# Half B's late FFN pairs from seven block products, with weight sums made during half A's FFN

## The chip, the cores and the metric

The kernel runs on one core of a Trainium2 chip. The metric is the device time of one launch in microseconds (us), as the median of several runs.

## The reference, cut to what matters

One decoder layer is computed in fp32 for a prompt (1024 tokens) and eight short samples (8 x 4 tokens) that share weights. Two branches (RG-LRU and chunked gated linear attention) are merged; then comes the FFN, which the change touches:

```python
h2 = _rmsnorm(x, norm2_g) * (1.0 + sc2) + sh2
f1, f2 = jnp.split(h2 @ ffn_w1, 2, axis=-1)          # D_MODEL 1024 -> 2 x D_FF, D_FF = 2816
x = x + gt2 * ((jax.nn.silu(f1) * f2) @ ffn_w2)
```

## The kernel before, in words

Activations lie with features on the 128 partitions and tokens along the free axis. The tokens are worked in two halves one after the other: half A has 512 prompt tokens, half B has the other 512 and the 32 of the samples, 544. `B` keeps a product in two PSUM banks of 272 columns each. In names in the traces, `a` or `b` behind a tile's name is the half.

Every fp32 product is three fp32r matmuls (`gemm`, lines 355 to 357): high part of the weight by high part of the activation, high by low, low by high. Activations are stored as high and low part side by side in one tile. Weights come from DRAM on SyncE's queue (`load_raw`, three buffers) and are split when they arrive (`split_w`): ScalarE writes the high part (line 136), VectorE the difference (line 137), into an `hl` tile (three buffers). Splits are issued with raised priority (`AHEAD`), so that they stand some 70 instructions earlier than their place in the code.

The FFN has 22 pairs; `pair` (from line 1079) makes one block of 128 features of `f1` and of `f2`, each from eight 128-row blocks of `h2` (24 matmuls for each 512 or 272 columns). It then takes the tanh on ScalarE, two VectorE products, and the split of the result into an `fa` tile (ScalarE line 1099, VectorE line 1100). `back` runs the output projection, the second norm and the first eleven pairs, the first four of them (`EARLY`) on the two parts of the half separately (`ffn1_first`), the others on the whole (`ffn1`). Then `ffn2` runs: eight columns, each of 33 matmuls over the eleven `fa` tiles, with weights in two loads of six and five blocks. The second eleven pairs and the second `ffn2` follow in the main program.

What decides the order: the program is written as generators that are advanced in turn; a scheduler then lists the instructions of each engine by priority, as far as tiles are free. At run time each engine works its list strictly in order and waits on semaphores. Tiles come from pools: 17 `S` tiles (wide activations, `fa` among them), 6 `t` tiles (temporaries), one `m2t` tile, 3 `raw`, 3 `hl`; in PSUM half A has 6 tiles of one bank, half B 3 of two. GpSimd has little to do: a few products and copies in the branches, and outputs on its DMA queue (lines 788, 833, 1147).

## Time and profile before

| | us |
|---|---|
| median of 3 runs (2044.50 to 2046.26) | 2045.36 |
| the profiled execution | 2041.18 |
| its span in the trace | 2039.2 |

The page of the profile gives busy times and shares for each engine (PE is TensorE, PEld its weight loads, DVE VectorE, ACT ScalarE, POOL GpSimd, SP SyncE), then the span in 40 slices. Timeline rows give start, duration, engine, line, operation, tiles written and read, and in brackets how long the engine was idle before and what ended that. The stages that matter here, by the timeline: half A's first four FFN pairs on its first part end at about 653 us, its pairs on the whole begin at about 674, its first `ffn2` at about 750, its second eleven pairs end at about 930; half B's FFN begins at about 1655 us and runs to 2026 us.

### The profile page before, as it was taken

The numbers are of one execution on the slowest core, as the hardware profiler recorded it, in microseconds if no ns is written. First come the engines' busy times: TensorE is split into PE (matmuls) and PEld (weight loads), VectorE is DVE, ScalarE is ACT, GpSimd is POOL, SyncE is SP. The second block draws the span as 40 slices with busy tenths as digits, with TensorE's granted clock in tenths as the row PEclk, the third lists the DMA queues.
The fourth block names the chain that finished last, engine by engine and source line by source line (L and its number), as shares of the span: only waits on it lengthen the run. The fifth ranks groups of instructions, "written<-read, shape, count | busy, mean of one in ns | idle before, by whom it ended". The sixth has DMA issues, their size and how long they took to land. (4 is left out here: it accounts for less than half of the span.)

```text
span 2039.2 us, 31760 instructions
## 1 busy us (share of the span) xinstructions
PE 2005.9 (98%) x13306; PEld 1808.0 (89%) x13306; DVE 1096.8 (54%) x1768; ACT 799.0 (39%) x1117; POOL 76.1 (4%) x130
## 2 busy tenths in 40 slices
PE   8999999999999999999999999999999999999997
PEld 5887877777899888888899999999999999999997
DVE  5647586544358433446473597764334773333346
ACT  3534375533335322333352355653322442222232
POOL 0101001000000000000010011010000000000000
PEclk9999999999999999999999999999999999999998
DMA  8323223334344323232412312323233542232243
GB/s 305 105 92 125 88 94 116 102 119 159 93 153 158 124 78 119 93 132 84 149 63 87 126 53 94 109 89 104 73 92 108 177 134 87 72 105 93 82 121 123
DMA packets 74638, 228.39 MB, mean 112 GB/s; under 512 B 8704, under 2 KB 16768, under 8 KB 74496
## 3 DMA queue, kind: packets, MB, share of 16 engines
q1 hardware_dynamic: 71536, 217.38, 32.8%
q0 software_dynamic: 2416, 8.44, 1.1%
q8 instruction: 104, 1.70, 0.3%
q10 hardware_dynamic: 544, 0.56, 0.1%
q14 instruction: 38, 0.31, 0.0%
HBM read 217.11 MB, written 9.23 MB: 111 GB/s over the span
## 5 line engine op out<-in xcount | busy, mean ns | idle before, releaser
L357 PE MATMUL f3psb<-fab,f3b_hl 128*128 128x272 f32 x352 | 101.4, 288 | 0.0
L355 PE MATMUL f3psb<-fab,f3b_hl 128*128 128x272 f32 x352 | 101.3, 288 | 0.0
L356 PE MATMUL f3psb<-fab,f3b_hl 128*128 128x272 f32 x352 | 100.9, 287 | 0.0
L136 ACT ACTIVATE f3b_hl<-f3b_raw 128x768 fp32r<-128x768 f32 (+1 forms) x45 | 35.7, 793 | 88.6 <-PE f3psb L357 58.3
L355 PE MATMUL f3psa<-faa,f3a_hl 128*128 128x512 f32 x176 | 68.7, 390 | 0.0
L357 PE MATMUL f3psa<-faa,f3a_hl 128*128 128x512 f32 x176 | 68.5, 389 | 0.0
L356 PE MATMUL f3psa<-faa,f3a_hl 128*128 128x512 f32 x176 | 68.5, 389 | 0.0
L355 PEld LDWEIGHTS f3psb<-fab,f3b_hl 128*128 128x128 f32 x352 | 66.4, 189 | 0.0
L357 PEld LDWEIGHTS f3psb<-fab,f3b_hl 128*128 128x128 f32 x352 | 66.2, 188 | 0.0
L356 PEld LDWEIGHTS f3psb<-fab,f3b_hl 128*128 128x128 f32 x352 | 66.1, 188 | 0.0
L137 DVE TENSOR_TENSOR f3b_hl<-f3b_raw,f3b_hl 128x768 fp32r<-128x768 f32 (+1 forms) x45 | 40.1, 892 | 35.2 <-ACT f3b_hl L136 34.8
L136 ACT ACTIVATE f3a_hl<-f3a_raw 128x768 fp32r<-128x768 f32 (+1 forms) x32 | 25.4, 793 | 84.3 <-PE f3psa L357 47.9
L137 DVE TENSOR_TENSOR f3a_hl<-f3a_raw,f3a_hl 128x768 fp32r<-128x768 f32 (+1 forms) x32 | 28.5, 892 | 39.1 <-ACT f3a_hl L136 38.4
L355 PE MATMUL uxpsb<-h1b,uxpsb_hl 128*128 128x272 f32 x160 | 47.0, 293 | 0.1
L357 PE MATMUL uxpsb<-h1b,uxpsb_hl 128*128 128x272 f32 x160 | 46.4, 290 | 0.0
L355 PE MATMUL ugpsb<-h1b,ugpsb_hl 128*128 128x272 f32 x160 | 46.2, 289 | 0.0
L357 PE MATMUL ugpsb<-h1b,ugpsb_hl 128*128 128x272 f32 x160 | 46.1, 288 | 0.0
L356 PE MATMUL uxpsb<-h1b,uxpsb_hl 128*128 128x272 f32 x160 | 45.9, 287 | 0.0
L356 PE MATMUL ugpsb<-h1b,ugpsb_hl 128*128 128x272 f32 x160 | 45.8, 286 | 0.0
L357 PEld LDWEIGHTS f3psa<-faa,f3a_hl 128*128 128x128 f32 x176 | 33.0, 188 | 7.0 <-DVE f3a_hl L137 0.2
L356 PEld LDWEIGHTS f3psa<-faa,f3a_hl 128*128 128x128 f32 x176 | 33.0, 188 | 6.9
L355 PEld LDWEIGHTS f3psa<-faa,f3a_hl 128*128 128x128 f32 x176 | 33.0, 188 | 6.8
(1477 smaller groups left out, 7129.0 us busy)
## 6 DMA issues: line engine op xcount, KB each, us to landing
ada<-in_ada_w SPq DMA_DIRECT2D x48, 512.0 KB, 5.3
f3b_raw<-in_ffn SPq DMA_DIRECT2D x23, 384.0 KB, 3.1
f3b_raw<-in_ffn SPq DMA_DIRECT2D x22, 320.0 KB, 2.9
woa_raw<-in_w_out SPq DMA_DIRECT2D x13, 512.0 KB, 3.5
wob_raw<-in_w_out SPq DMA_DIRECT2D x13, 512.0 KB, 3.2
f3a_raw<-in_ffn SPq DMA_DIRECT2D x16, 384.0 KB, 3.1
uxpsa_raw<-in_w_in SPq DMA_DIRECT2D x10, 512.0 KB, 3.6
ugpsa_raw<-in_w_in SPq DMA_DIRECT2D x10, 512.0 KB, 3.6
```

Source lines behind the costliest of these rows:

```text
L136: act.activation(hl[:, 0, :n], raw[:, :n], AF.Copy)
L137: dve.tensor_sub(hl[:, 1, :n], raw[:, :n], hl[:, 0, :n].bitcast(F32))
L355: pe.matmul(out, wh, x[:, o:o + w], start=st, stop=False)
L356: pe.matmul(out, wh, x[:, N + o:N + o + w], start=False, stop=False)
L357: pe.matmul(out, wl, x[:, o:o + w], start=False, stop=en)
```

## The change

Half B's pairs from number 6 (`PLAIN`) on, sixteen of them, are made by `pair7`. A pair's weights are seen as 2 x 2 blocks (`f1` and `f2`, 128 outputs each, by two halves of 512 input rows), and `h2` as 2 x 2 blocks too (those halves by two halves of 272 tokens). Seven block products of 12 matmuls with 272 columns (four 128-row blocks times three parts) replace eight, by way of sums of weight blocks and of activation blocks:

- `make_sums` (32 steps, one for each of the 16 pairs and half of the columns) makes the four sums of weight blocks on GpSimd in the one `m2t` buffer, splits them (ScalarE line 187, VectorE line 188 of the new file) into two `S` tiles, and stores them to DRAM from GpSimd's queue. It is advanced during half A's FFN.
- `mixed` and `mixed_last` make the sums of `h2` blocks in half B, with three fourths of them during the first six pairs.
- `pair7` loads `qa` and `qe` on SyncE's queue and splits them as before (512 and 256 KB), and the stored sums `qc` (1 MB), `qb` and `qd` (512 KB each) on GpSimd's queue, which need no split. Products `x`, `y` share a PSUM tile of two banks (`xy`), `v`, `z` another (`wz`). In between, ScalarE and VectorE take what is done so far out of the banks (`e`, `u2`, `u4`, `f2`, `f12`).

```diff
@@ -28,6 +28,7 @@
 LEVELS = (64, 32, 16, 8, 4, 2, 1)
 EPS = 1e-6
 EARLY = 4
+PLAIN = 6
 AHEAD = 70
 def starts_of(w):
     return [min(i, w - P) for i in range(0, w, P)]
@@ -162,6 +163,31 @@
         def __getitem__(s, at):
             rows, u, cols = at
             return s.of[u][rows, cols]
+
+
+    dp = ctx.enter_context(tc.tile_pool(name="dp", bufs=1, space=bass.MemoryType.DRAM))
+    sums = {}
+
+    def make_sums(fs):
+
+        for f in fs:
+            sums[f] = dp.tile([P, 2, 4, 512], F32R, tag=f"sum{f}", name=f"sum{f}")
+            for i in range(2):
+                q = tp.tile([P, 2 * 544], F32, tag="m2t", name=f"sq{f}{i}", bufs=1)[:, :1024].rearrange("p (s n) -> p s n", s=4)
+                c = slice(256 * i, 256 * i + 256)
+                w = [I["ffn1"][2 * f + u].rearrange("p (k n) -> p k n", k=2)[:, :, c] for u in range(2)]
+                for u, k, at in (0, 0, 1), (0, 1, 3), (1, 0, 2), (1, 1, 0):
+                    pool.dma_start(q[:, at], w[u][:, k])
+                pool.tensor_add(q[:, 0], q[:, 2], q[:, 0])
+                pool.tensor_add(q[:, 2], q[:, 1], q[:, 2])
+                pool.tensor_add(q[:, 1], q[:, 1], q[:, 0])
+                pool.tensor_add(q[:, 3], q[:, 3], q[:, 1])
+                yield 0.0
+                hi, lo = (S(f"s{u}{f}{i}", F32R)[:, :1024].rearrange("p (s n) -> p s n", s=4) for u in "hl")
+                act.activation(hi, q, AF.Copy)
+                dve.tensor_sub(lo, q, hi.bitcast(F32))
+                for u, t in (0, hi), (1, lo):
+                    pool.dma_start(sums[f][:, u, :, c], t)
 
     def w_in_tile(t, name):
         return load_w(I["w_in"][t], 1024, name)
@@ -322,6 +348,7 @@
             s.parts = [(0, 256, 0, 0), (256, 256, 0, 256)] if hf == 0 else [(0, 272, 0, 0), (272, 272, 1, 0)]
             s.adas = ada_rest() if hf == 0 else iter(())
             s.early = {}
+            s.seven = s.hf == 1
             s.lr_raw = None
 
         def ada(s, n):
@@ -1100,6 +1127,108 @@
             dve.tensor_sub(lo, tg, hi.bitcast(F32))
             yield w * 24 / 2400.0
 
+        def mixed(s):
+
+            N, w = s.N, s.N // 2
+            s.t1, s.t2, s.t3, s.t4 = [], [], [], []
+            whole = lambda h, o, n: (h[:, o:o + n].bitcast(F32), h[:, N + o:N + o + n].bitcast(F32))
+            for j in range(4):
+                n = f"{s.n}{j}"
+                hs, gs = T("mh" + n), T("mg" + n)
+                dve.tensor_add(hs[:, :N], *whole(s.h2[j], 0, N))
+                dve.tensor_add(gs[:, :N], *whole(s.h2[4 + j], 0, N))
+                yield
+                h0, h1, g0, g1 = hs[:, :w], hs[:, w:N], gs[:, :w], gs[:, w:N]
+                dve.tensor_sub(h0, h0, h1)
+                dve.tensor_sub(h1, h1, g1)
+                dve.tensor_add(g1, h0, g1)
+                dve.tensor_sub(g0, g0, g1)
+                t34 = S("mt" + n, F32R)
+                if j % 2 == 0:
+                    t2 = S("mu" + n, F32R)
+                for dst, at, src, to in (t34, 0, h1, s.t3), (t34, N, g0, s.t4), (t2, j % 2 * N, g1, s.t2):
+                    split(dst[:, at:at + N], src, w)
+                    to.append((dst[:, at:at + w], dst[:, at + w:at + N]))
+                    yield
+
+        def mixed_last(s):
+            N, w = s.N, s.N // 2
+            for j in range(4):
+                h = s.h2[j]
+                hs = T(f"ml{s.n}{j}")
+                dve.tensor_add(hs[:, :N], h[:, :N].bitcast(F32), h[:, N:2 * N].bitcast(F32))
+                dve.tensor_sub(hs[:, :w], hs[:, :w], hs[:, w:N])
+                hi, lo = h[:, w:N], h[:, N + w:2 * N]
+                act.activation(hi, hs[:, :w], AF.Copy)
+                dve.tensor_sub(lo, hs[:, :w], hi.bitcast(F32))
+                s.t1.append((hi, lo))
+
+        def quarter(s, k0, c):
+            N, w = s.N, s.N // 2
+            return [(h[:, c * w:c * w + w], h[:, N + c * w:N + c * w + w]) for h in s.h2[k0:k0 + 4]]
+
+        def pair7(s, f, a):
+
+            n, N, w = f"{s.n}{f}", s.N, s.N // 2
+            d = sums[f]
+
+            def prod(out, hl, u, rhs, first, last):
+                for k, (xh, xl) in enumerate(rhs):
+                    c = u * 512 + k * P
+                    wh, wl = hl[:, 0, c:c + P], hl[:, 1, c:c + P]
+                    pe.matmul(out, wh, xh, start=(first and k == 0), stop=False, skip_group_check=True)
+                    pe.matmul(out, wh, xl, start=False, stop=False, skip_group_check=True)
+                    pe.matmul(out, wl, xh, start=False, stop=(last and k == 3), skip_group_check=True)
+
+            def load(at, name):
+                hl = wp.tile([P, 2, 1024], F32R, tag="hl", name=name + n + "_hl", bufs=3)
+                pool.dma_start(hl[:, :, :512 * len(at)].rearrange("p u (s n) -> p u s n", n=512), d[:, :, at.start:at.stop])
+                return hl
+
+            xy, wz = mm("xy" + n), mm("wz" + n)
+            x, y = (xy[:, 0, :w], xy[:, 1, :w]) if s.hf else (xy[:, 0, :w], xy[:, 0, w:N])
+            v, z = (wz[:, 0, :w], wz[:, 1, :w]) if s.hf else (wz[:, 0, :w], wz[:, 0, w:N])
+            eu, vf, tg, f2 = T("eu" + n), T("vf" + n), T("tg" + n), T("ff" + n)
+            e, u2 = eu[:, :w], eu[:, w:N]
+            u4, f12 = vf[:, :w], vf[:, w:N]
+            ha = load_w(I["ffn1"][2 * f], 1024, "qa" + n)
+            prod(x, ha, 0, s.quarter(0, 0), True, True)
+            with tc.high_priority(AHEAD + 20):
+                act.activation(e, x, AF.Copy)
+            hc = load(range(1, 3), "qc")
+            prod(y, hc, 0, s.t2, True, True)
+            with tc.high_priority(AHEAD + 20):
+                dve.tensor_sub(u2, y, e)
+            yield w * 24 / 2400.0
+            prod(x, ha, 1, s.quarter(4, 0), False, True)
+            prod(v, hc, 1, s.t3, True, True)
+            with tc.high_priority(AHEAD + 20):
+                dve.tensor_add(u4, u2, v)
+            act.activation(tg[:, :w], x, AF.Tanh, scale=0.5)
+            dve.scalar_tensor_tensor(tg[:, :w], tg[:, :w], 1.0, x, op0=OP.add, op1=OP.mult)
+            yield w * 24 / 2400.0
+            hb = load(range(0, 1), "qb")
+            raw = load_raw(I["ffn1"][2 * f + 1][:, 512:], 512, "qe" + n)
+            with tc.high_priority(AHEAD):
+                act.activation(hb[:, 0, 512:], raw[:, :512], AF.Copy)
+                dve.tensor_sub(hb[:, 1, 512:], raw[:, :512], hb[:, 0, 512:].bitcast(F32))
+            prod(z, hb, 0, s.t1, True, True)
+            with tc.high_priority(AHEAD + 20):
+                dve.tensor_sub(f2[:, w:N], u4, z)
+            prod(v, hb, 1, s.t4, False, True)
+            dve.tensor_add(f2[:, :w], u2, v)
+            yield w * 24 / 2400.0
+            hd = tp.tile([P, 2 * 544], F32R, tag="m2t", name="qd" + n, bufs=1)[:, :1024].rearrange("p (u n) -> p u n", u=2)
+            pool.dma_start(hd, d[:, :, 3])
+            prod(z, hd, 0, s.quarter(4, 1), False, True)
+            with tc.high_priority(AHEAD + 20):
+                dve.tensor_sub(f12, z, u2)
+            act.activation(tg[:, w:N], f12, AF.Tanh, scale=0.5)
+            dve.scalar_tensor_tensor(tg[:, w:N], tg[:, w:N], 1.0, f12, op0=OP.add, op1=OP.mult)
+            dve.tensor_mul(tg[:, :N], tg[:, :N], f2[:, :N])
+            split(a, tg[:, :N], N)
+            yield w * 12 / 2400.0
+
         def ffn1_first(s, part, n):
             for f in range(n) if part[0] == 0 else range(n - 1, -1, -1):
                 if part[0] == 0:
@@ -1111,7 +1240,7 @@
                 s.act = []
             for f in range(11 * g + f0, 11 * g + 11):
                 a = S(f"fa{s.n}{f}", F32R)
-                yield from s.pair(f, s.whole, a)
+                yield from s.pair7(f, a) if s.seven and f >= PLAIN else s.pair(f, s.whole, a)
                 s.act.append(a)
 
         def ffn2(s, g, part, acc=None):
@@ -1162,9 +1291,21 @@
             next(f)
             mix(s.norm2(p1, a1), f)
             drain(f)
-            drain(s.ffn1_first(p1, EARLY))
-            drain(s.ffn1(0, EARLY))
-            drain(s.ffn2(0, s.whole))
+            m = s.mixed() if s.seven else make
+            for _ in s.ffn1_first(p1, EARLY):
+                next(m, None)
+            f = s.ffn1(0, EARLY)
+            if s.seven:
+                for _ in range(2 * (PLAIN - EARLY)):
+                    next(f)
+                    for _ in range(3):
+                        next(m, None)
+                drain(m)
+                s.mixed_last()
+            for _ in f:
+                next(make, None)
+            for _ in s.ffn2(0, s.whole):
+                next(make, None)
 
         def branches(s, before):
             s.y_a, s.os_ = [None] * NR, []
@@ -1203,6 +1344,7 @@
         for _ in range(n):
             pe.matmul(idle, src[:, :P], src[:, :512], start=True, stop=True, skip_group_check=True)
 
+    make = make_sums(range(PLAIN, NF))
     A.begin()
     load_later()
     derive()
@@ -1210,6 +1352,8 @@
     up1 = A.ffn1(1)
     for _ in range(16):
         next(up1)
+        next(make, None)
+    drain(make)
     B.load_x()
     drain(up1)
     acc = [ACC("3a")]
```

Three places in the engines' lists (a row: line, operation, tile written, tiles read, shape; the number behind a tile's name tells instances apart).

ScalarE before, from the tanh of pair 9 in half A into the first `ffn2` (`f1ps` products, `fta` tanh, `faa` 9 and 10 the activations, `f3a...` the weights of the `ffn2` columns):

```order
L1093 ACTIVATE fta9None0_5807<-f1psa9None0_5777 128x512
L136 ACTIVATE f3a0000_hl_5913<-f3a0000_raw_5911 128x768
L1099 ACTIVATE faa9_5776<-fta9None0_5807 128x512
L136 ACTIVATE f3a0001_hl_5936<-f3a0001_raw_5934 128x640
L1093 ACTIVATE fta10None0_5874<-f1psa10None0_5844 128x512
L136 ACTIVATE f3a0010_hl_5958<-f3a0010_raw_5956 128x768
L1099 ACTIVATE faa10_5843<-fta10None0_5874 128x512
L136 ACTIVATE f3a0011_hl_5981<-f3a0011_raw_5979 128x640
L136 ACTIVATE f3a0020_hl_6003<-f3a0020_raw_6001 128x768
L136 ACTIVATE f3a0021_hl_6026<-f3a0021_raw_6024 128x640
```

ScalarE now, at the last `fa` tiles of the same stage (`sh` is the high part of a step's sums, `sq` its buffer; 120 is the first half of pair 12):

```order
L187 ACTIVATE sh120_5840<-sq120_5795 128x1024
L187 ACTIVATE sh121_5886<-sq121_5846 128x1024
L1126 ACTIVATE faa7_5855<-fta7None0_5902 128x512
L187 ACTIVATE sh130_5938<-sq130_5893 128x1024
L187 ACTIVATE sh131_5984<-sq131_5944 128x1024
L1126 ACTIVATE faa8_5953<-fta8None0_6000 128x512
L187 ACTIVATE sh140_6036<-sq140_5991 128x1024
L187 ACTIVATE sh141_6082<-sq141_6042 128x1024
L1126 ACTIVATE faa9_6051<-fta9None0_6098 128x512
L187 ACTIVATE sh150_6134<-sq150_6089 128x1024
L187 ACTIVATE sh151_6180<-sq151_6140 128x1024
L1126 ACTIVATE faa10_6149<-fta10None0_6196 128x512
```

Rows of line 187 of the steps 60 to 151 (20 of them, the first right behind the copy for `fa` 3 on its first part) now stand ahead of the copy that makes `fa` 10; two each stand between the copies of `fa` 6 to 10, and the splits of three `ffn2` columns stand ahead of them. Of the other 12, all but the last two stand among the later splits of weights; the last but one stands ahead of the split of `f1` 18, and the last behind `f2` 18, ahead of the tanh of `f1` 17, six copies of `fa` tiles and the split of `f1` 19.

GpSimd now, one step and the beginning of the next, where it had nothing to do (`sq` is the buffer of the step, `sum6` the place in DRAM):

```order
L180 DMA sq61_5266<-in_ffn1 128x256 x4
L181 TENSOR_TENSOR sq61_5266<-sq61_5266 128x256
L182 TENSOR_TENSOR sq61_5266<-sq61_5266 128x256
L183 TENSOR_TENSOR sq61_5266<-sq61_5266 128x256
L184 TENSOR_TENSOR sq61_5266<-sq61_5266 128x256
L190 DMA sum6_5219<-sh61_5305 128x4x256
L190 DMA sum6_5219<-sl61_5306 128x4x256
L180 DMA sq70_5312<-in_ffn1 128x256 x4
```

The loads of the next step stand behind both stores of this one, and the buffer `sq` is the same memory in every step.

TensorE in half B, in pair 7 (`xyb7` and `wzb7` are the two PSUM tiles, `qab7`, `qcb7`, `qbb7` the weights, `mtb`, `mub` the sums of `h2`): the end of `y`, the rest of the first product on `v`, and the start of `x`'s second half,

```order
L1179 MATMUL xyb7_15665<-mub2_15328,qcb7_hl_15689 128x272
L1180 MATMUL xyb7_15665<-mub2_15328,qcb7_hl_15689 128x272
L1181 MATMUL xyb7_15665<-mub2_15328,qcb7_hl_15689 128x272
L1180 MATMUL wzb7_15666<-mtb1_15191,qcb7_hl_15689 128x272
L1181 MATMUL wzb7_15666<-mtb1_15191,qcb7_hl_15689 128x272
L1179 MATMUL wzb7_15666<-mtb2_15327,qcb7_hl_15689 128x272
L1180 MATMUL wzb7_15666<-mtb2_15327,qcb7_hl_15689 128x272
L1181 MATMUL wzb7_15666<-mtb2_15327,qcb7_hl_15689 128x272
L1179 MATMUL xyb7_15665<-h2b04_14532,qab7_hl_15673 128x272
L1180 MATMUL xyb7_15665<-h2b04_14532,qab7_hl_15673 128x272
L1181 MATMUL xyb7_15665<-h2b04_14532,qab7_hl_15673 128x272
```

and some rows later the end of `x`'s second half, the end of the first product on `v`, and the start of `z`:

```order
L1180 MATMUL xyb7_15665<-h2b07_14586,qab7_hl_15673 128x272
L1181 MATMUL xyb7_15665<-h2b07_14586,qab7_hl_15673 128x272
L1179 MATMUL wzb7_15666<-mtb3_15403,qcb7_hl_15689 128x272
L1180 MATMUL wzb7_15666<-mtb3_15403,qcb7_hl_15689 128x272
L1181 MATMUL wzb7_15666<-mtb3_15403,qcb7_hl_15689 128x272
L1179 MATMUL wzb7_15666<-h2b00_14473,qbb7_hl_15731 128x272
L1180 MATMUL wzb7_15666<-h2b00_14473,qbb7_hl_15731 128x272
L1181 MATMUL wzb7_15666<-h2b00_14473,qbb7_hl_15731 128x272
L1179 MATMUL wzb7_15666<-h2b01_14478,qbb7_hl_15731 128x272
```

In the first piece five rows of `v` stand between the last row of `y` and the first of `x`, which share a tile; in the second, `z` follows directly on `v`, in the same tile. Ahead of `y`, four rows of `v` stand behind the last row of the first half of `x`. Before, a pair was 48 rows for `f1` and 48 for `f2`, each in a tile of its own.

## The prediction

> **What bounds the kernel now.** The page of the profile was read first: its busy shares, then its 40 slices.
>
> ```profile
> span 2039.2 us, 31760 instructions
> PE 2005.9 (98%) x13306; PEld 1808.0 (89%) x13306; DVE 1096.8 (54%) x1768; ACT 799.0 (39%) x1117; POOL 76.1 (4%) x130
> PEclk9999999999999999999999999999999999999998
> GB/s 305 105 92 125 88 94 116 102 119 159 93 153 158 124 78 119 93 132 84 149 63 87 126 53 94 109 89 104 73 92 108 177 134 87 72 105 93 82 121 123
> ```
>
> TensorE is busy for 98% of the span at its full clock, and no other engine comes near it. Fewer matmuls would show in full; whatever makes TensorE wait would show in full too. What one matmul costs is read from the windows (span of the window, then busy time and count of PE, PEld, DVE, ACT, POOL, then clock, DMA share, GB/s), since the durations in the groups overlap.
>
> ```profile
> 700.00:745.00 45.00, 45.00 (x200) 37.27 (x199) 17.08 (x20) 12.30 (x16) 0.00 (x0) 1.00 0.28 89
> 1655.00:1684.00 29.00, 29.00 (x235) 29.00 (x234) 15.75 (x25) 11.98 (x19) 0.00 (x0) 1.00 0.44 146
> 1684.00:1708.00 24.00, 24.00 (x195) 24.00 (x194) 9.06 (x10) 6.47 (x9) 0.00 (x0) 1.00 0.28 88
> 1840.00:1960.00 120.00, 120.00 (x967) 120.00 (x966) 45.08 (x51) 31.74 (x42) 0.00 (x0) 1.00 0.25 82
> ```
>
> The first is half A's FFN: 45.00/200 = 0.225 us for a matmul of 512 columns, so a pair (48 of them) takes 10.8 us. The last is half B's: 120.00/967 = 0.124 us for 272 columns. GpSimd does nothing in any of them.
>
> **What is removed.** Each of B's 16 late pairs loses one block product in eight, 12 matmuls: 16 x 12 x 0.124 = **-23.8 us**.
>
> **What is added in half A.** There are 32 steps, one per pair and half. A step is four loads and four additions on GpSimd, a copy on ScalarE, a subtraction on VectorE, two stores from GpSimd's queue. All steps share one buffer, and the next step's loads stand on GpSimd's queue behind the store of the low part. So the steps run in single file, and the question is the length L of one. Its rows:
>
> ```profile
> 723.50 1.06 ACT L136 ACTIVATE f2a9None_hl<-f2a9None_raw 128x1024 fp32r<-128x1024 f32 x1 [3.86 <-issue]
> 724.59 1.23 DVE L137 TENSOR_TENSOR f2a9None_hl<-f2a9None_raw,f2a9None_hl 128x1024 fp32r<-128x1024 f32 x1 [3.61 <-ACT f2a9None_hl L136]
> 69.12 2.40 POOL L647 TENSOR_TENSOR qea<-qa,e0a 128x1024 f32<-128x1024 f32 x1 [47.88 <-ACT e0a L646]
> L833 POOL DMA_DIRECT2D out_gla_s<-s0b x8 | 4.3, 538 | 55.4 <-DVE s0b L826 34.8 <-DVE qmb L796 20.6
> L1147 POOL DMA_DIRECT2D out_yb<-yb x4 | 2.9, 718 | 532.4 <-DVE yb L1144 532.2
> out_gla_p<-stb POOLq DMA_DIRECT2D x4, 128.0 KB, 2.1
> out_gla_s<-s0b POOLq DMA_DIRECT2D x8, 512.0 KB, 3.4
> ```
>
> The weight split has the shapes of the step's own: the low part starts 1.09 us after the copy and lasts 1.23. GpSimd takes 0.54 to 0.72 us to issue a DMA; the low part's store has 512 pieces, which no row shows, so I take 0.8. Then four loads: three issues of 0.55 and 2.1 from the fourth's issue to its landing, 3.75. They follow two 512 KB stores on the same queue (3.4 us each to land), for which I add 0.7, between nothing and 1.3. Four additions of 256 columns at a quarter of 2.40 are 2.4; with some waiting for VectorE (below) 2.9. Five handovers between engines, 0.4. **L = 1.09 + 1.23 + 0.8 + 3.75 + 0.7 + 2.9 + 0.4 = 10.9 us.** The smallest terms alone (1.09 + 1.23 + 0.54 + 3.72 + 2.4) give 9.0; the largest (issues of 0.72 with 1.2 for the store, 1.3 behind the stores, additions of 3.4/4 and 0.85 each, as the row of 3.39 below) some 13.3.
>
> One file of 32 steps would do no harm if nobody stood behind it. But ScalarE takes its instructions in order, and the order above has the first 20 step copies ahead of the copy that makes `fa` 10. All three opened columns of `ffn2` end in matmuls with `fa` 10. So TensorE's fourth column starts only after the twentieth step. In the profile:
>
> ```profile
> 652.33 0.42 ACT L1099 ACTIVATE faa<-fta 128x256 fp32r<-128x256 f32 x1 [0.35 <-DVE fta L1097]
> 751.45 0.62 ACT L1099 ACTIVATE faa<-fta10None 128x512 fp32r<-128x512 f32 x1
> 772.89 0.39 PE L355 MATMUL f3psa<-faa,f3a_hl 128*128 128x512 f32 x1
> 773.09 0.75 DVE L1052 SCALAR_TENSOR_TENSOR xma<-f3psa,gains,xma 128x512 f32<-128x512 f32 x1 [1.80 <-PE f3psa L357]
> 882.22 0.58 ACT L1093 ACTIVATE fta17None<-f1psa17None 128x512 f32<-128x512 f32 x1
> 897.33 0.39 PE L355 MATMUL f1psa19None<-h2a,f1a19None_hl 128*128 128x512 f32 x1
> ```
>
> The first step copy follows the row of 652.33 (it and the addition it needs are ready by then), so at about 653.0; the twentieth at 653.0 + 19L. Behind it come its own copy and low part (2.3), the low part of `fa` 10 (0.7), the last nine matmuls (9 x 0.225 = 2.0) and a handover, 5.2 together. Before, the third column's result is read at 773.09, and the fourth column begins with the matmul at 772.89. Delay there: 653.0 + 19L + 5.2 - 772.9 = **19L - 114.7**. The other 12 steps go in between three half columns or one pair at a time, 10.8 to 11.2 us of TensorE, close to L, so there the file neither loses nor gains much. The last copy stands ahead of the tanh of `f1` 17 and six `fa` copies, and these ahead of the weights of `f1` 19, whose first matmul was at 897.33: 653.0 + 31L + 1.06 + 0.58 + 6 x 0.62 + 2.3 - 897.3 = 31L - 236.6. The larger of the two is the delay: for L = 10.9 they are 92 and 101. **A costs +101 us**; for L = 9.0 it is 56 (the first formula), for 13.3 it is 176. TensorE has no reserve from which to win this back.
>
> What TensorE's clock does in these gaps is a cost too:
>
> ```profile
> 2020.00:2039.20 19.20, 8.79 (x66) 8.51 (x64) 8.61 (x29) 1.89 (x4) 0.00 (x0) 0.71 0.17 58
> ```
>
> Where TensorE is idle for over half of a window, the mean clock is 0.71. Between the first step copy and the fourth column TensorE had 120 us of work (653 to 772.9) and will have 212 us of time, so the gaps per step are some 5 us. If all its matmuls there ran at half clock, 240 us of work would not fit in 212: +28 us. I count nothing, because that clock would close the gaps that bring it about. [...]
>
> **What is added in half B.** Products now share two PSUM tiles, and each tile is waited for as a whole. What such a turn takes is in the timeline:
>
> ```profile
> 1655.57 0.41 ACT L1099 ACTIVATE fab<-ftb 128x272 fp32r<-128x272 f32 x1
> 1659.54 0.29 PE L357 MATMUL f2psb<-h2b,f2b_hl 128*128 128x272 f32 x1
> 1659.86 0.44 DVE L1097 TENSOR_TENSOR ftb<-ftb,f2psb 128x272 f32<-128x272 f32 x1 [0.32 <-PE f2psb L357]
> ```
>
> 0.32 us from the last matmul's start to its reader, 0.44 for the reader, an estimated 0.06 back: 0.82. Matmuls of other products that stand in between cover part of it. By the order, `y` has four rows between it and the copy's last input (0.41 for ScalarE's copy makes a turn of 0.79, less five starts of 0.124: 0.17 left), `x`'s second half five (0.82 less six: 0.07), `z` none (0.82 less one: 0.70), the products with `t4` and `qd` six and five (together 0.07). **1.0 us a pair, +16 us** in all; nothing if the reader starts before the others' rows are through, at most 2.7 a pair (four whole turns less some cover), +43, if no cover holds.
>
> VectorE must also make the sums of `h2`:
>
> ```profile
> 1662.10 0.43 DVE L1100 TENSOR_TENSOR fab<-ftb,fab 128x272 fp32r<-128x272 f32 x1
> 1841.30 0.72 DVE L1100 TENSOR_TENSOR fab<-ftb11None,fab 128x544 fp32r<-128x544 f32 x1
> ```
>
> 12 sums of 544 columns at 0.72, and 20 sums and differences and 16 low parts of 272 at 0.43 make 24.1 us, in the 53 us of the second and third windows above, where it has 15.75 + 9.06 = 24.8 busy. 49 of 53 still fits, but splits of weights will come late now and then: +3 (0 to 10). A pair loads 2.75 MB rather than 1 MB, in 84 x 0.124 + 1 = 11.4 us, some 250 GB/s. The span's first slice reached 305 GB/s, so this can be carried. ScalarE's split of `qe` waits for `qb` behind it on GpSimd's queue and stands ahead of the copy for `y`: +3, from 0 to 16 us.
>
> **The sum.** From the profiled execution's 2041.2 us: + 101 - 23.8 + 16 + 3 + 3 = 2140. The runs' median, 2045.4, lies 4 us above that execution, and I carry the 4 us over: **2144 us** for the runs of the changed kernel.
>
> **The rivals.**
> (1) *Faster: A's making is hidden and B's turns are covered.* It ends on the other side if L is under 114.7/19 = 6.0 us, because then `fa` 10 is not late. For it speaks that GpSimd is 4% busy and DMA a quarter; against it, that L's smallest terms sum to 9.0. Price: no 101 and no 16: 2144 - 117 = 2027 us. 3%.
> (2) *Level: A hidden, B's turns as worked out*: 2045 - 2 = 2043. 2%.
> (3) *GpSimd's additions are locked out by VectorE.* The rows:
>
> ```profile
> 70.18 2.44 DVE L137 TENSOR_TENSOR vpsa_hl<-vpsa_raw,vpsa_hl 128x1024 fp32r<-128x1024 f32 x1
> 71.49 3.39 POOL L655 TENSOR_TENSOR kea<-kea,ka 128x1024 f32<-128x1024 f32 x1
> ```
>
> The split that takes 1.23 us alone took 2.44, ending about 1.1 after GpSimd's addition of 69.12 did; the next addition took 3.39 rather than 2.40. Each waits out the other's instruction. If every step meets one more VectorE instruction of 1.23 than I allowed, L is 12.1, the delay 138, the time 2181. Against it: while TensorE waits, VectorE has little to do. 14%. [...]
> (4) *Clock at half in A's gaps*: +28, 2172. 6%.
> (5) *B's loads on GpSimd's queue come late* (1.6 us a pair beyond the 3): +25, 2169. 12%.
>
> **How the numbers follow.** The forecast (L between 9.7 and 11.9, B within 10 us) has 63%, and is the likeliest. Rivals 3 to 5 lie above it. The lowest bounds of A and B together give 2041 + 56 - 21 = 2076, the highest over 2250, but two ends at once are unlikely. The range of 2093 to 2212 runs from L = 9.4 with nothing else (19L - 114.7 = 64, B at -14) to L = 12.3 with B at +22; it leaves out rivals 1 and 2 and the ends of 3 and 5, some 15%. A measurement of this kernel tells about 0.2%, 4 us, from no change. Faster is rival 1 (3%), within 0.2% is rival 2 (2%), slower the rest (95%).
>
> **What would show it.** In the changed profile: TensorE gaps of about 5 us between 660 and 865, ended by a copy or low part of `fa` 6 to 10; 20 step copies about 10.9 us apart; GpSimd busy or waiting throughout; `f1` 19's first matmul near 998. In B, some 0.7 us of idle ahead of each `z` and little elsewhere, and 192 fewer matmuls. I am wrong if the step copies lie under 7.6 us apart, if step copies come apart but TensorE goes on (the order on ScalarE read wrongly), or if B's pairs take over 13 us.

## The result and the profile after

The changed kernel takes **2252.4 us** (median, 2250.5 to 2253.7) against 2044.9 us before: a ratio of 1.101 (95% interval 1.100 to 1.103), 207 us more. The forecast was 2144 us, with a range up to 2212: the direction was right, the size only half of it. Comparisons below leave out one run, the second of `e8_file_spread` (2123.3 us), in which the granted clock was 0.91 rather than 0.99.

The page of the profile after, its span, busy times and granted clock:

```profile
span 2250.1 us, 32312 instructions
PE 2054.9 (91%) x13114; PEld 1814.6 (81%) x13114; DVE 1178.6 (52%) x1944; ACT 837.1 (37%) x1197; POOL 323.4 (14%) x498
PEclk9999999999999965788899999999999999999998
```

TensorE has the 192 matmuls fewer that were expected (13,306 before), and its share of the span fell from 98% to 91%: it waits. The clock's digits below 9 in slices 15 to 20 say where: a slice is 56 us, so from 788 to 1125 us. The windows show it closer (span; busy time and count of PE, PEld, DVE, ACT, POOL; clock, DMA share, GB/s):

```profile
650.00:760.00 110.00, 95.52 (x488) 79.79 (x486) 42.59 (x58) 32.58 (x47) 47.62 (x71) 0.94 0.61 177
760.00:870.00 110.00, 46.61 (x145) 33.02 (x146) 24.09 (x28) 18.47 (x23) 53.39 (x80) 0.69 0.54 145
870.00:980.00 110.00, 59.62 (x219) 44.60 (x219) 27.42 (x32) 19.59 (x23) 54.61 (x83) 0.75 0.57 160
980.00:1090.00 110.00, 91.83 (x333) 70.17 (x333) 32.74 (x35) 23.14 (x27) 48.51 (x74) 0.87 0.63 183
```

Before, 45 us of half A's FFN held 200 matmuls, so 110 us would hold 489. Now the second window holds 145. The waits of TensorE between 640 and 1140 us (line waited for: total, times, longest) name the cause:

```profile
PE f3psa L382 <- ACT faa L1126: 83.9, 5, 20.8
PE f3psa L382 <- ACT f3a_hl L137: 13.3, 5, 8.2
PE f1psa10None L382 <- ACT f1a10None_hl L137: 6.1, 1, 6.1
```

83.9 us go to the high parts of `fa` tiles for the first `ffn2`, the rest mostly to weight splits of single products. Both are ScalarE instructions that stand behind step copies. The twentieth copy, the copy of `fa` 10 right behind it and the matmuls that waited for that:

```profile
917.94 1.06 ACT L187 ACTIVATE sh<-sq 128x1024 fp32r<-128x1024 f32 x1 [12.21 <-POOL sq L184]
918.90 0.61 ACT L1126 ACTIVATE faa<-fta10None 128x512 fp32r<-128x512 f32 x1
919.57 1.22 PE L382 MATMUL f3psa<-faa,f3a_hl 128*128 128x512 f32 x2 [20.79 <-ACT faa L1126]
```

From the first matmul of half A's FFN to the first of half B's the time grew from 999.2 to 1203.3 us, **+204.1**; half B's FFN grew from 400.1 to 403.5, **+3.4**; 2.7 us are lost ahead of the output projection of half A, and 0.7 behind half B's FFN.

How late the end of single products of half A is against before (last matmul's start, less the 2.7 us), from the timelines:

| product | before, us | after: late by |
|---|---|---|
| `f1` 10 | 744.8 | 33.7 |
| `ffn2` column 1, first matmul | 750.5 | 35.0 |
| `ffn2` column 4, first matmul | 772.9 | 148.4 |
| `f1` 11 | 815.5 | 156.4 |
| `f1` 17 | 880.8 | 189.5 |
| `f1` 19 to `f2` 21 | 902.5 to 929.7 | 202.7 |

The step itself, in the timeline of GpSimd after, with the ScalarE and VectorE rows that belong to it:

```profile
803.52 0.79 POOL L190 DMA_DIRECT2D sum<-sh  x1 [1.39 <-ACT sh L187]
804.78 0.78 POOL L190 DMA_DIRECT2D sum<-sl  x1 [0.47 <-DVE sl L188]
805.55 2.19 POOL L180 DMA_DIRECT2D sq<-in_ffn  x4
813.64 0.72 POOL L181 TENSOR_TENSOR sq<-sq 128x256 f32<-128x256 f32 x1 [5.90 <-DMA sq<-in_ffn]
814.43 0.72 POOL L182 TENSOR_TENSOR sq<-sq 128x256 f32<-128x256 f32 x1
815.24 0.72 POOL L183 TENSOR_TENSOR sq<-sq 128x256 f32<-128x256 f32 x1
816.04 0.72 POOL L184 TENSOR_TENSOR sq<-sq 128x256 f32<-128x256 f32 x1
816.79 1.06 ACT L187 ACTIVATE sh<-sq 128x1024 fp32r<-128x1024 f32 x1 [12.20 <-POOL sq L184]
817.88 1.23 DVE L188 TENSOR_TENSOR sl<-sq,sh 128x1024 fp32r<-128x1024 f32 x1 [11.19 <-ACT sh L187]
```

The single file is there as forecast, but one round of it is 14.2 us on average (31 rounds from 655.0 to 1094.2), not 10.9. The step copies of the whole file (shortest, median and longest in ns, then the first and last start):

```profile
L187 ACT ACTIVATE sh<-sq x32: 1041/1056/1061, 655.0 to 1094.2; 128x1024 fp32r<-128x1024 f32 x32
```

Link by link, as means over the steps:

| link | forecast, us | measured, us |
|---|---|---|
| copy to start of low part | 1.09 | 1.09 |
| low part | 1.23 | 1.23 |
| store of the low part, issue | 0.8 | 0.77 |
| first to fourth load's issue | 1.65 | 1.67 |
| **fourth load's issue to the first addition** | **2.8** (2.1 + 0.7) | **5.84** |
| four additions | 2.9 | 3.16 |
| handovers | 0.4 | 0.40 |
| sum | 10.9 | 14.2 |

One term is wrong by 3.0 us in each step; the others together by 0.3.

### The profile page after: what moved, and what is told of

Its sections match the earlier page's. It is cut to its first block, busy times and chain, and to the rows that moved or that the text cites. A ratio compares the mean times of both kernels' runs of the same rounds, so it can differ in the third digit from the quotient of the medians.

```text
span 2250.1 us, 32312 instructions
## 1 busy us (share of the span) xinstructions
PE 2054.9 (91%) x13114; PEld 1814.6 (81%) x13114; DVE 1178.6 (52%) x1944; ACT 837.1 (37%) x1197; POOL 323.4 (14%) x498
## 5 line engine op out<-in xcount | busy, mean ns | idle before, releaser
L188 DVE TENSOR_TENSOR sl<-sq,sh 128x1024 fp32r<-128x1024 f32 x32 | 39.2, 1226 | 306.4 <-ACT sh L187 306.4
L382 PE MATMUL f3psa<-faa,f3a_hl 128*128 128x512 f32 x176 | 75.4, 433 | 97.1 <-ACT faa L1126 83.9
L187 ACT ACTIVATE sh<-sq 128x1024 fp32r<-128x1024 f32 x32 | 33.8, 1057 | 329.6 <-POOL sq L184 329.6
L382 PEld LDWEIGHTS f3psa<-faa,f3a_hl 128*128 128x128 f32 x176 | 36.2, 208 | 108.8 <-ACT faa L1126 86.4
L180 POOL DMA_DIRECT2D sq<-in_ffn x128 | 70.9, 571 | 62.8 <-DVE tia L970 61.7
L384 PE MATMUL f3psa<-faa,f3a_hl 128*128 128x512 f32 x176 | 74.8, 425 | 4.2 <-DVE f3a_hl L138 4.1
L383 PE MATMUL f3psa<-faa,f3a_hl 128*128 128x512 f32 x176 | 75.0, 426 | 0.5
L1185 POOL DMA_DIRECT2D qcb_hl<-sum x16 | 11.3, 705 | 347.1 <-PE f1psb5None L384 219.8
L190 POOL DMA_DIRECT2D sum<-sh x32 | 25.2, 786 | 209.6 <-ACT sh L187 206.9
L384 PEld LDWEIGHTS f3psa<-faa,f3a_hl 128*128 128x128 f32 x176 | 36.6, 208 | 14.4 <-DVE f3a_hl L138 6.8
L181 POOL TENSOR_TENSOR sq<-sq 128x256 f32<-128x256 f32 x32 | 23.5, 734 | 169.2 <-DMA sq<-in_ffn 169.2
L382 PE MATMUL uxpsb<-h1b,uxpsb_hl 128*128 128x272 f32 x160 | 47.0, 294 | 0.1
L384 PE MATMUL uxpsb<-h1b,uxpsb_hl 128*128 128x272 f32 x160 | 46.4, 290 | 0.0
L382 PE MATMUL ugpsb<-h1b,ugpsb_hl 128*128 128x272 f32 x160 | 46.2, 289 | 0.0
```

What stands on the lines that cost most here:

```text
L180: pool.dma_start(q[:, at], w[u][:, k])
L187: act.activation(hi, q, AF.Copy)
L188: dve.tensor_sub(lo, q, hi.bitcast(F32))
L190: pool.dma_start(sums[f][:, u, :, c], t)
L382: pe.matmul(out, wh, x[:, o:o + w], start=st, stop=False)
L383: pe.matmul(out, wh, x[:, N + o:N + o + w], start=False, stop=False)
```

## The experiments

### Half A and half B apart

Two kernels, each with one part of the change. In the first no sums are made, and half B loads as many bytes from the plain weights.

```diff
-    make = make_sums(range(PLAIN, NF))
+    make = iter(())
...
-            d = sums[f]
+            d = I["ffn1"][2 * f:2 * f + 2].rearrange("u p n -> p u n").bitcast(F32R)
...
```

> No sums are made in half A; half B's late pairs load as many bytes in the same pieces from the plain first FFN weights (so the FFN of half B is computed from other numbers). Theory (half A's making costs the time, 204 us, and half B nearly nothing): 2045 + 3.5 = about 2048 to 2050, half A's FFN as long as before. Rival (half B's pairs lose much of the time, and half A's part is smaller): well over 2060. Rival (the making hurt half B as well, by leftovers in the queues): under 2045.

Measured: 2043.6 us, ratio 1.000 (0.9985 to 1.0016). That is under the 2045 of the last rival, but by less than the interval; half B's FFN is 1.6 us longer than before, against 3.4 in the change, whose one wait for `qcb` takes 2.2 us where this run has 0.4. In the second, half B has plain pairs:

```diff
-            s.seven = s.hf == 1
+            s.seven = False
```

> The sums are made and stored in half A as in the change, but half B uses plain pairs and never reads them. Theory: 2045 + 204 = about 2249, step copies 14.2 us apart. Rival (the two parts hurt each other): clearly less than 2249, under 2235.

Measured: 2247.4 us, ratio 1.100 (1.097 to 1.102), step copies 14.2 us apart. So half A's making is the whole cost, and half B's seven products neither gain nor lose anything clear of the interval: the two parts add up. In e1_b_alone's late pairs 24 us of gaps between matmuls stand against the 23.8 us of matmuls saved. TensorE's longest row of waits there:

```profile
PE wzb L1179 <- DVE vfb L1206: 7.4, 14, 0.5
```

That is `z` waiting for `u4` in its own tile. From matmul start to matmul start, the gaps ahead of `z` come to 9.9 us in 16 pairs, 0.62 each.

### What makes the loads late

> As e2_a_alone, without the stores of the sums (they are not kept). Theory (the loads of a step wait behind the 1 MB that the step before has just stored): from the fourth load's issue to the first addition 5.84 us fall to about 2.2, and the stores' own issues leave the file, so a step takes about 9.5 us; by 19L and 31L that makes half A about 68 us longer, 2113. Rival (the loads in pieces of 1 KB, or the weights on SyncE's queue beside them, are slow by themselves): 5 us stay, a step takes about 12.5 us, 2195 or more. Rival (TensorE's lower clock, not the file, sets the time): no clear relation between step length and time.

```diff
-                for u, t in (0, hi), (1, lo):
-                    pool.dma_start(sums[f][:, u, :, c], t)
```

> As e2_a_alone, with the stores issued from ScalarE's queue rather than GpSimd's. Theory 1 (loads wait behind the stores because they share a queue): landing falls towards 2.5 us, a step takes about 10 us, 2120. Theory 2 (loads and stores share the DMA engines, whatever queue): landing stays near 5, a step takes about 13 us, 2210.

```diff
-                    pool.dma_start(sums[f][:, u, :, c], t)
+                    act.dma_start(sums[f][:, u, :, c].bitcast(F32), t.bitcast(F32))
```

Measured: 2197.2 us without the stores (ratio 1.075, 1.072 to 1.079), 2227.2 us with the stores on ScalarE's queue (1.090, 1.086 to 1.093). Both expectations of the first theory fail: steps of 11.9 us rather than 9.5 without the stores, 12.7 rather than 10 with the stores elsewhere (the second theory of e4_stores_act, a shared path whatever the queue, had 13). The loads are slow without any store too, which speaks for the rival, SyncE's weights beside them. Within one kernel the steps part into two kinds. GpSimd in e3_no_stores, an early step and one from the stretch in which TensorE hardly moves and no weights come:

```profile
666.75 2.15 POOL L180 DMA_DIRECT2D sq<-in_ffn  x4 [2.65 <-DVE sl L188]
673.89 0.73 POOL L181 TENSOR_TENSOR sq<-sq 128x256 f32<-128x256 f32 x1 [4.99 <-DMA sq<-in_ffn]
...
846.05 2.15 POOL L180 DMA_DIRECT2D sq<-in_ffn  x4 [2.65 <-DVE sl L188]
850.58 0.72 POOL L181 TENSOR_TENSOR sq<-sq 128x256 f32<-128x256 f32 x1 [2.38 <-DMA sq<-in_ffn]
```

and a step from the same stretch of the changed kernel, with its stores:

```profile
846.49 2.20 POOL L180 DMA_DIRECT2D sq<-in_ffn  x4
852.31 0.72 POOL L181 TENSOR_TENSOR sq<-sq 128x256 f32<-128x256 f32 x1 [3.62 <-DMA sq<-in_ffn]
```

Sorting all steps by whether SyncE's queue moved over 50 KB between the first load's issue and the first addition gives, from the fourth issue to the first addition:

| | no weights beside | weights beside |
|---|---|---|
| no stores ahead (e3_no_stores) | 2.85 us (5 steps) | 4.59 us (26) |
| stores ahead on the same queue (the change) | 4.16 us (7) | 6.33 us (24) |
| stores on ScalarE's queue (e4_stores_act) | 4.15 us (4) | 5.36 us (27) |

By themselves the loads take 2.85 us, where the forecast had 2.1. Stores ahead of them add 1.3 us, weights beside them 1.7, both 3.5. Without weights the stores cost the same from either queue. Beside weights the step with its stores on ScalarE's queue looks 1 us shorter, but fewer weights came beside it, 610 KB on average against 906. Where over 900 KB came, it took 6.9 us (8 steps) against 6.5 (16); where less than 600 KB came, 4.4 (15) against 5.7 (5). A queue of their own for the stores thus helped here only where few weights came. What loads and stores share is more than the queue; whether it is the DMA engines or the memory isn't parted by these runs.

VectorE's splits come with the weights, so they could be what holds GpSimd's loads up instead. The trace of e3_no_stores speaks against it: in eight of its 26 steps beside weights VectorE did nothing between the fourth issue and the first addition, and these took 4.6 us on average, as all 26 did; in one of the five steps without weights it was busy for 2.7 us of that time, which was 2.86 us long, as in the other four.

### Does the file or the work cost?

The theory that stood: it costs that steps in file stand ahead of `fa` 10 and of weight splits, and not that their work is done. The first test is half as many steps, at the change's own pace (the last eight pairs, half B plain):

```diff
-    make = make_sums(range(PLAIN, NF))
+    make = make_sums(range(14, NF))
```

> As e2_a_alone, for the last eight pairs only (16 steps in single file, at the change's own pace). In the order all 16 step copies stand ahead of fa 8 to 10. Theory (the file sets when fa 10 and with it the fourth ffn2 column can go): 655 + 15 x 13.9 = 863 for the last step copy, the fourth column some 7 us behind it, at 870 against 773 before: +97, 2142. Rival (the cost goes with the work, half of e2_a_alone's 202): +101 too, but then spread evenly over the steps; told apart by where the delay stands: all of it at the fourth column by the theory, nothing after.

Measured: 2145.5 us, ratio 1.049 (1.047 to 1.052). The last step copy starts at 862.8 us, the fourth column is late by 102.4 us, and so, to a tenth of a microsecond, is every product behind it, as the theory has it (34 us of it stand already at `f1` 10, as in the change, since weight splits stand behind step copies too). But no step is left behind the fourth column, and 16 steps at half of e2_a_alone's cost would be 101 us too, so this run alone doesn't part the two; the next ones do.

```profile
PE f3psa L382 <- ACT faa L1126: 41.7, 3, 19.8
PE f3psa L382 <- ACT f3a_hl L137: 11.0, 3, 9.6
```

The second test keeps the change's step, again 16 of them, and begins one for each 20 us of matmul work. The counter that does it stands in place of the plain `next(make, None)`:

```diff
...
+    def along(g, every):
+        for got in g:
+            owed[0] += got
+            while owed[0] >= every:
+                owed[0] -= every
+                next(make, None)
+            yield got
```

> The change's own step (one buffer, loads behind the stores, some 14 us each), half B plain, but for eight pairs only (16 steps) and with a step begun for each 20 us of matmul work. In the order four step copies still stand close together near the first ffn2. Theory (placement decides, with the same step): 2045 to 2060, against some 98 us more (653 + 15 x 13.8 + 5.2 - 772.9 = 92) if 16 such steps stood ahead of fa 10. Rival (each step costs what it takes, wherever it stands): 16 x 6.4 = 102 more, 2147.

Measured: 2078.0 us in its first run alone, so there is no interval; its span is 2076.2 us, 37 us more than before. Half a microsecond is lost up to the end of the first pairs, 10.2 us at the first `ffn2` where four steps stand close, and the rest at the second `ffn2` and the beginning of half B. Spreading the same number of the same steps takes 68 us off the 105 of e10_file_eight, so a cost that is the same wherever a step stands is out; but the theory's 2045 to 2060 was missed too.

### A shorter step, spread, and half B's turns covered

Three kernels to see whether both costs can go. In half B, `x` shares a tile with `v` and `y` with `z`, and a pair's last two products are issued behind the first product of the next pair:

```diff
-            xy, wz = mm("xy" + n), mm("wz" + n)
+            xv = mm("xv" + n)
+            x, v = xv[:, 0, :w], xv[:, 1, :w]
...
             prod(x, ha, 0, s.quarter(0, 0), True, True)
...
+            if s.pend is not None:
+                yield from s.pend
+            yz = mm("yz" + n)
+            y, z = yz[:, 0, :w], yz[:, 1, :w]
...
+            def close():
+                prod(v, hb, 1, s.t4, False, True)
...
+                prod(z, hd, 0, s.quarter(4, 1), False, True)
...
+            s.pend = close()
```

> As e1_b_alone (no sums made in half A, half B's FFN computed from other numbers of the same size), but half B's products share PSUM tiles differently (x with v, y with z) and the last two products of a pair are issued behind the next pair's first one, so that 12 matmuls of another tile stand in nearly every turn. Theory (the seven products' gain of 23.8 us is eaten by the turns of shared tiles, 26 us): the excess between matmuls falls to about 8 us, and the time to about 2045 - 23.8 + 8 = 2029. Rival (the excess is due to weights that come late on GpSimd's queue): it stays, about 2044, or grows because qb is now needed sooner.

Measured: 2036.5 us, ratio 0.9965 (0.995 to 0.998). The turn of `z` is gone, gaps fall from 24 to 17 us rather than to 8, because other waits come up (TensorE, half B's pairs):

```profile
PE xvb L1182 <- DVE qab_hl L138: 3.7, 9, 0.6
PE yzb L1180 <- DMA qcb_hl<-in_ffn: 3.3, 5, 1.3
```

With the turns covered, the loads of 1 MB on GpSimd's queue and the split of `qa` are late. Theory and rival each have a share.

In half A, the step's buffer becomes a wide `S` tile with the low part written in its place, the next step's loads stand ahead of this step's stores, and a step is begun for each 9.6 us of matmul work:

```diff
-                q = tp.tile([P, 2 * 544], F32, tag="m2t", name=f"sq{f}{i}", bufs=1)[:, :1024].rearrange("p (s n) -> p s n", s=4)
+            q = S(f"sq{f}{i}")[:, :1024].rearrange("p (s n) -> p s n", s=4)
...
+            ahead = begin(*steps[k + 1]) if k + 1 < len(steps) else None
             yield 0.0
...
+            lo = q.bitcast(F32R)
```

> All sums are made and used. Half A: the buffer of a step is one of the wide S tiles (several in turn) with the low part written in its place, the next step's loads are issued ahead of this step's stores, and a step is begun for each 9.6 us of matmul work, on into the second ffn2. Half B as in e5_b_order. Theory (A's cost is the file of steps standing ahead of fa tiles and weights, not the work): step copies fall between fa copies, half A is as long as before within 5 us, and the time is that of e5_b_order, 2029 to 2034, faster than both kernels. Rival (the making costs by its DMA traffic, its VectorE and ScalarE work or the clock): half A 30 us or more longer, 2060 or more.

> Half A as in e6_both, half B with plain pairs that do not read the sums. Theory: half A as long as before within 5 us, 2045 to 2050, a step's own length about 8 us where nothing holds it. Rival (the work itself costs): 2075 or more.

Measured: 2084.1 us with both (ratio 1.020, 1.018 to 1.021) and 2094.5 us with half A's part alone (1.025, 1.023 to 1.027). Half A is about 49 us longer in both, so the theory fails as put, and the rival's 30 us or more come true. But the marks show where: in e7_a_spread no product of the first eleven pairs is late at all (0.0 at `f1` 10; 0.9 in e6_both), 16 us are lost at the first `ffn2`, none in the next eleven pairs, the rest at the second `ffn2` and the beginning of half B. TensorE's waits in e7_a_spread:

```profile
PE f3psa L402 <- DVE f3a_hl L138: 9.2, 7, 2.8
PE f3psa L400 <- ACT f3a_hl L137: 7.1, 3, 3.1
PE lrpsb L585 <- DVE xma L1097: 7.0, 1, 7.0
```

Beside pairs a step has 10.9 us of matmuls around it; in the first `ffn2` there are eight steps beside its eight columns of 7.5 us. That led to the last three: steps beside pairs only, and as many late pairs as there is room for, ten (20 steps), nine (18), and ten with steps begun sooner (8.3 us of matmul work for each rather than 9.0). The cut is against e6_both; the last sums of `h2` also move, to just ahead of the late pairs:

```diff
-            drain(s.ffn2(0, s.whole) if s.seven else along(s.ffn2(0, s.whole), 9.6))
+            drain(s.ffn2(0, s.whole))
...
-    make = make_sums(range(PLAIN, NF))
+    make = make_sums(range(LATE, NF))
```

> As e6_both, for the last ten pairs only (20 steps), with steps begun only beside half A's FFN pairs, none beside its ffn2 columns (where e6_both and e7_a_spread lost their time). Theory (a step costs nothing where a pair's 10.9 us of matmuls lie between two steps): half A as long as before within 4 us, half B 10/16 of what e5_b_order won (8.5 us), so 2045 - 5 = about 2040, ratio 0.997 to 0.999. Rival (each step costs about 1.5 us anyhow, 48 us in 32 steps of e6_both): 2045 + 30 - 5 = 2070.

> As e9_ten for nine pairs (18 steps): the last two steps of e9_ten, which stood close together ahead of the split of f2 21, fall away. Theory (a step that stands behind a whole pair costs nothing, one crowded against the next costs what it is late): half A not longer at any mark; half B wins 9/16 of 8.5 = 4.7 us; 2044 - 5 = 2039, ratio 0.9975 to 0.999, faster than both kernels by a little. Rival (late steps cost wherever they end): a delay of some 8 us at the last pairs stays, ratio about 1.002.

> As e9_ten (ten pairs, 20 steps), with a step begun for each 8.3 us of matmul work rather than 9.0, so that the last step's split stands one pair earlier; three times two steps stand in one pair. Theory: the three crowded pairs give some us each only if the two steps together take over 10.9 us with the slack built up before; half A 0 to 10 us longer, 2039 to 2050. Rival as for e11_nine.

| kernel | ratio (95% interval) | half A's FFN to half B's | half B's FFN |
|---|---|---|---|
| e9_ten | 1.0021 (1.0010 to 1.0032) | +8.6 us | -5.1 us |
| e12_ten_early | 1.0018 (1.0006 to 1.0030) | +14.7 us | -3.3 us |
| e11_nine | 0.9985 (0.9974 to 0.9997) | +0.1 us | -1.9 us |

The theory of e9_ten is missed (half A 8.6 us longer rather than under 4), and so is its rival (30). Eighteen of its steps delay no product (0.1 us at every mark up to `f1` 21, 924.3 us before); the last two stand close together ahead of the split of `f2` 21, whose last matmul is 8.5 us late. Nearly all of the loss is there, 6.0 us in the wait and the rest in slower matmuls behind it:

```profile
PE f2psa21None L402 <- ACT f2a21None_hl L138: 6.0, 1, 6.0
```

Without them, in e11_nine, half A costs nothing: the work of 18 of these shorter steps is free where it stands well. Half B then gains 1.9 us of the 4.7 expected, since the loads are late there too (`yzb` waits 4.9 us for `qcb`, against 2.0 in e9_ten). e12_ten_early three times has two steps in one pair and loses 10.1 us at `f1` 19 and `f2` 19; the other 4.6 of its 14.7 are lost behind half A's second `ffn2`, with no new wait, where two windows of 100 us have a granted clock of 0.98 and 0.97 rather than 1.00 (0.992 over the whole profiled run, against 0.996 in e9_ten's). e11_nine is the one version that makes all it uses and is faster than both kernels, than the kernel before by 0.15% (between 0.03 and 0.26%), about as little as these runs can tell.

## Why the prediction was wrong, point by point

**The bound and the saving** were right: 192 matmuls fell away and TensorE's waits show in full.

**The step's length was the error.** The term "three issues of 0.55 and 2.1 from the fourth's issue to its landing, 3.75", with 0.7 for the stores ahead "between nothing and 1.3", allowed 2.8 us from the fourth issue to the landing; it took 5.84. The row of 2.1 us was a transfer of 128 KB with little beside it (three of its four instances, with 58 to 61 GB/s moved in all, about its own bytes; the fourth, in a window with 262 GB/s, took 6.2), and it was one output store, not the last of four loads. Three things make up the 3.0 us: the loads alone took 2.85 rather than 2.1 (+0.75); the 1 MB of stores ahead cost 1.3 rather than 0.7 (+0.6); and in 24 of 31 rounds weights came beside them, which with the stores ahead cost 2.2 (6.33 less 4.16), 1.7 on average over all rounds. The prediction weighed the stores and put the weights at nothing, without a word on them; that is the largest part. Its top value, 13.3, stayed under the 14.2 measured, and the terms that it names for it add up to only 12.9.

**The formulas on that length held**, the second in part by luck. The first 19 rounds took 262.9 us from 655.0, so the fourth column was due 655.0 + 262.9 + 5.2 - 772.9 = 150 us late; it was 148.4 + 2.7 = 151. With L = 14.2 in 31L - 236.6 the prediction's own line gives 204, and the last matmul of `f1` 19 was 202.7 + 2.7 = 205 us late. But two errors offset each other there. The order shown ahead of the prediction is said to have six copies of `fa` tiles behind the last step copy; there are five (12 to 16; that of `fa` 11 stands ahead of it), 0.52 us apart, so `f1` 19 began 5.1 us behind that copy (1094.2 to 1099.3) and not 7.7. The product then took 8.7 us from its first matmul to its last rather than 5.2, since eight of its matmuls were 0.38 to 0.43 us apart and three more gaps were longer. The order of ScalarE read ahead of time was thus right but for one copy, and each error of 1 us in L cost 31. The waits for `fa` 6 to 10 came too, but as five of 6 to 21 us, one for two steps, where gaps of some 5 us a step were forecast.

**Half B** was put at -2 us and was +3.4, and alone +1.6. The turn of `z` was forecast at 0.70, with 0.06 for the way back to TensorE that no row showed, and is 0.62 on average: 0.69 to 0.70 in 14 of the 16 pairs, where `z` started 0.05 to 0.06 us behind the end of `u4`, and 0.11 in the other two. `y` and the others are near their values too. Not forecast was a gap of some 0.1 us ahead of the second matmul of each product that follows such a turn (about 7 us in 16 pairs). VectorE's sums of `h2`, put at +3, cost 0.3: the gaps in that stretch are 3.1 us, before 2.8.

**The rivals.** GpSimd locked out by VectorE, 14%: four additions took 3.16 us on average and 3.38 at most, so that was not it. A slower clock, 6%: the clock did fall to 0.69 to 0.87 in three of half A's windows, but it explains only a few us of the end. Its +28 us took half the clock, which no row shown ahead of the prediction has (the lowest mean there is 0.71). In the changed kernel the granted clock is 0.50 over the longest gap and 0.51 over the 4.8 us behind it, in which the matmuls start 0.43 us apart rather than 0.225:

```profile
921.93 0.63 PE L383 MATMUL f3psa<-faa,f3a_hl 128*128 128x512 f32 x1
922.36 0.63 PE L384 MATMUL f3psa<-faa,f3a_hl 128*128 128x512 f32 x1
922.78 0.63 PE L382 MATMUL f3psa<-faa,f3a_hl 128*128 128x512 f32 x1
```

For the nine matmuls behind `fa` 10 that is 2 us. From 924.4 us on the clock is 1.00 again. TensorE had time to spare between steps (46.6 us busy of 110 in the second window), so a slow clock mostly filled gaps there. At the end it shows in the first 6.0 us of `f1` 19, with a clock of 0.51: some 0.2 us more for each of the eight matmuls makes 1.6 of the 3.5 us more that it took. No run changed the clock alone. Loads of half B late, 12%: one wait of 2.2 us in the change; it became a cost only when e5_b_order had covered the turns.

## What to carry to other kernels

Work given to an idle engine was free here only where no one waited in order behind its results (e11_nine's 18 steps cost half A 0.1 us, the change's 32 steps 204): look at the lists of the engines that take them in (here ScalarE's copy), and count how much matmul work stands between two of them. A chain through one buffer multiplies every error in its length by the number of rounds (3.3 us by 31 here); take the landing of a transfer from a row with the same traffic beside and ahead of it, not from a lone one (2.1 us in the row, 5.84 in the step from the same issue to the first addition). Where tiles are waited for as a whole, choose what shares a tile by who is read when (`z` lost 0.62 us a pair behind `u4`; in e5_b_order that turn was gone).

## What the runs showed of the hardware

The instruction that waited for four loads of 128 KB in pieces of 1 KB started 2.85 us after the fourth's issue with nothing beside them (e3_no_stores), 4.2 us behind 1 MB of stores, whether these were on the same queue (4.16, the change) or another (4.15, e4_stores_act), 4.6 us beside weight loads on SyncE's queue (e3_no_stores), and 6.3 us with both, the stores on the loads' queue (the change). In the changed kernel, a store of 512 pieces took GpSimd 0.78 us to issue, a load of 128 pieces 0.55. TensorE's granted clock there was 0.50 over a gap of 20.8 us, 0.51 over the 4.8 us behind it, and 1.00 over the next 1.6 us.
